# Cross-covariance attention on one core: the first V transfer moved behind the fourth unit of Q and K, and the first casts and transposes of V moved to later steps

## The chip, the core and the metric

The kernel runs on one core of a Trainium2 chip. A core has a matrix engine (TensorE, PE), a vector engine (VectorE, DVE), a scalar engine (ScalarE, ACT), a general one (GpSimd, POOL) and SyncE (SP), which here issues all DMA transfers. Each engine works through its own list of instructions in order and waits on semaphores for the others. The metric is device microseconds of one execution; before the change the median of five runs is 132.33 us.

## The reference

Q, K and V have shape 8 x 12 x 512 x 64 in float32: 96 heads, each with 512 rows of 64 numbers.

```python
Q_norm = Q / (np.linalg.norm(Q, axis=-2, keepdims=True) + 1e-10)
K_norm = K / (np.linalg.norm(K, axis=-2, keepdims=True) + 1e-10)
attn = np.einsum('bhnd,bhne->bhde', Q_norm, K_norm)
attn = np.exp(attn - np.max(attn, axis=-1, keepdims=True))
attn = attn / (np.sum(attn, axis=-1, keepdims=True) + 1e-10)
return np.einsum('bhnd,bhde->bhne', V, attn).astype(np.float32)
```

The attention matrix is one over features, 64 x 64 a head. It comes out of a sum over all 512 rows of Q and K, and V (512 x 64) is then multiplied by it.

## The kernel before

The heads are taken in 24 units of four heads. A unit of Q or of K is one transfer of 512 KB into a tile of 128 partitions. V comes in 12 transfers of 1 MB, numbered w, each holding two units; a V unit is numbered v. The output leaves in 512 KB stores, one for each unit (the last one in two halves). All loads and stores stand in one queue on SP, in the order in which the program calls load_qk (L69), load_v (L75) and store (L79). Up to eight transfers are in flight: from the ninth on, each waits for the landing of the one eight places ahead of it, and, where it reuses a buffer, for the engine that read it last.

The order of the work is written out by hand: the program has a manual schedule, and each engine runs its instructions in the order of the calls in the loop over steps (L229 to L258). In step s these parts stand one after another:

- load_qk for unit s + 3, V loads (L232) and stores (L235) as they come due
- cast_v (L89): a V unit is cast to bf16, one half on ACT and the other on DVE (L96, one instruction on each)
- cast_q (L82) for unit s + 1 on DVE
- normalise (L141) for unit s - 2: sum, reciprocal and multiply on DVE
- grams (L98) for unit s: 64 small matmuls on PE that give Q and K products and their squared norms together
- norms (L110): four DVE instructions that read the diagonal out of PSUM, and a power on POOL (L120); keep_kq (L105), a copy on ACT; scale_k (L122) on POOL
- logits (L129) for unit s - 1, four transposes on PE; scale_q (L133) on DVE; exps (L137) on ACT
- cast_k (L86) for unit s + 1 on DVE
- outs (L179): 16 matmuls on PE and two copies on ACT for an output unit; at most one a step, from step 4 on
- doubled (L173) for unit s - 2: a matmul on PE and a copy on ACT
- clear (L214), a copy of zeros on ACT, in the first steps
- vtrans (L149) for the V units that this step cast: eight transposes on PE into the one buffer of ps_v, and an evacuation on ACT (L159)

The number of outputs that should be done by step s is outs_by(s) (L62), the whole part of (s - 2) * 9 / 10. It is 0 up to step 3 and 1 at step 4. Before the change the V units to be cast in step s run from nt, the first not yet transposed, to n1 + 1, with n1 = outs_by(s) (L238); step 0 has none. So step 1 takes units 0 and 1, steps 2 and 3 take none, and step 4 takes unit 2. The first V load is called ahead of the loop (L227), the second in step 0 (L232).

After the loop a second one (L265 to L284) does the last six outputs; there four V units are transposed in float32 straight from the loaded tile (vtrans_f32, L161), and the copies are shared between ACT and DVE.

Of the kernel before, what the change touches and what calls it, by code (L numbers as in the profile page):

```python
# [27 lines left out]
def kernel(  # L28
# [10 lines left out]
    U = B * H // HU  # L39
# [22 lines left out]
    def outs_by(s):  # L62

        return max(0, (s - 2) * 9 // 10)
# [10 lines left out]
    def load_v(w):  # L75
        vf[w] = vp.tile([128, 2 * R * D], F32, name="vf")
        nc.sync.dma_start(out=vf[w], in_=Vf[w])

    def store(u, g=slice(0, SV)):  # L79
        nc.sync.dma_start(out=Of[u][:, g], in_=so[u][:, g].rearrange("p s t d -> p s (t d)"))  # L80
# [8 lines left out]
    def cast_v(v):  # L89

        w, i = divmod(v, 2)
        if i == 0:
            vb[w] = vbp.tile([128, A, TP, 2 * D], BF16, name="vb")
        x = vf[w].rearrange("p (a t d) -> p a t d", a=A, d=2 * D)
        for t, copy in ((2 * i, nc.scalar.copy), (2 * i + 1, nc.vector.tensor_copy)):
            copy(vb[w][:, :, t], x[:, :, t])  # L96
# [52 lines left out]
    def vtrans(v):  # L149

        w, i = divmod(v, 2)
        ps = ps_v.tile([128, A, 2, 128], BF16, name="vps")
        for t in range(2):
            for a in range(A):
                nc.tensor.transpose(ps[:, a, t, :], vb[w][:, a, 2 * i + t, :], identb)  # L155

        if i == 0:
            vt[w] = vtp.tile([128, TP, 128, A], BF16, name="vt")
        nc.scalar.copy(vt[w][:, 2 * i:2 * i + 2], ps.rearrange("p a t c -> p t c a"))  # L159
# [19 lines left out]
    def outs(u, copies=(nc.scalar.copy, nc.scalar.copy)):  # L179
        s = so[u] = sop.tile([128, SV, TP, 2 * D], F32, name="so")  # L180
        a = abuf[u % len(abuf)]
        v = vt[u // 2][:, :, u % 2 * 64:(u % 2 + 1) * 64]
        for g in range(SV):
            po = ps_o.tile([128, TP, 2 * D], F32, name="po")
            for t in range(TP):
                for x in range(2):
                    h = 2 * g + x
                    nc.tensor.matmul(  # L188
                        po[MV * x:MV * (x + 1), t, :], v[:, t, NP * h:NP * (h + 1), :].rearrange("p c a -> p (c a)"),
                        a[:, h].rearrange("p a d -> p (a d)"), tile_position=(0, MV * x),  # L190
                    )
            copies[g](s[:, g], po)  # L192
# [21 lines left out]
    def clear(i):  # L214

        nc.scalar.copy(abuf[i].rearrange("p h a d -> p (h a d)"), zeros)
# [4 lines left out]
    def on(f, u):  # L221
        if 0 <= u < U:
            f(u)

    on(cast_q, 0)
    on(cast_k, 0)
    load_v(0)  # L227
    nv, nst, nt = 1, 0, 0
    for s in range(U):  # L229
        n0, n1 = outs_by(s - 1), outs_by(s)  # L230
        on(load_qk, s + LOAD_AHEAD)
        while nv < min(U, n1 + 5) // 2:  # L232
            load_v(nv)
            nv += 1
        while nst < n1 - 3:  # L235
            store(nst)
            nst += 1
        new = range(nt, n1 + 2) if s >= 1 else ()  # L238
        for v in new:
            cast_v(v)  # L240
        on(cast_q, s + 1)
        on(normalise, s - 2)
        on(grams, s)
        on(norms, s)
        on(keep_kq, s)
        on(scale_k, s)
        on(logits, s - 1)
        on(scale_q, s - 1)
        on(exps, s - 1)
        on(cast_k, s + 1)  # L250
        for v in range(n0, n1):
            outs(v)
        on(doubled, s - 2)
        if 6 <= s + 5 < len(abuf):
            clear(s + 5)
        for v in new:
            vtrans(v)
            nt = v + 1  # L258
# [59 lines left out]
```

## Time and profile before

| | |
|---|---|
| median of 5 runs | 132.33 us (131.15 to 134.85) |
| profiled execution, own time | 133.27 us |
| its span, first to last instruction | 131.5 us |
| busy: DVE / ACT / PE / POOL | 95.8 / 91.5 / 90.5 / 64.1 us |
| moved by DMA | 50.67 MB, 385 GB/s over the span |
| first V transfer, from its issue to its landing | 9.97 us |
| V transfers, median from issue to landing | 12.5 us |
| mean granted clock of PE | 0.883 |

The profile is one execution. A row of the timeline gives the start in us from the span's start, the duration in us, the engine, the source line, the operation, what it writes and reads, the shapes, and the number of instructions merged into the row; in brackets stands how long the engine had been idle and what ended the wait. "SPq" rows are issues of transfers, not their movement. A landing can be read from SP: the issue of a transfer that was held up starts just after the landing of the one eight places ahead. Busy shares are averages over stages with different limits, so a wait counts only where nothing else lies beside it.

### The profile page before, as it was taken

What the parts mean: (1) busy time and instruction counts of PE and PEld (TensorE: products, weight loads), DVE (VectorE), ACT (ScalarE), POOL (GpSimd) and SP (SyncE); (2) the same over time, 40 slices, a digit from 0 to 9 for tenths busy, and PEclk for the clock granted to TensorE, in tenths of its full rate; (3) what the DMA queues carried; (4) which work ended last, traced back from release to release, by engine and by line L of the source; (5) the groups of instructions that cost most, each with busy time, mean ns of one, the idle gap of its engine ahead of it and who ended that gap; (6) DMA issues with size and microseconds to landing.
All of it is one profiled execution on the core that took longest, in us unless ns stands there. A gap on an engine that the chain in (4) does not pass through costs nothing.

```text
span 131.5 us, 5389 instructions
## 1 busy us (share of the span) xinstructions
PE 90.5 (69%) x2232; PEld 70.2 (53%) x2232; DVE 95.8 (73%) x366; ACT 91.5 (70%) x171; POOL 64.1 (49%) x57
## 2 busy tenths in 40 slices
PE   0146346779968759866994799682897758979630
PEld 0135244657846548644863587461675646867420
DVE  0460855898698996994798979983979698478840
ACT  7610564357899999994978288987689968677530
POOL 4023172698258882671668447763545657140000
PEclk9999999999999995995589658999779985699995
DMA  4999999999999999999999999999999999976775
GB/s 141 383 415 417 424 406 414 401 425 399 416 412 399 441 391 410 426 403 411 427 393 412 411 424 409 409 427 405 413 423 409 409 414 413 407 289 224 282 273 206
DMA packets 15208, 50.67 MB, mean 385 GB/s; under 512 B 1360, under 2 KB 1360, under 8 KB 13648
## 3 DMA queue, kind: packets, MB, share of 16 engines
q1 hardware_dynamic: 15184, 50.34, 95.8%
q8 instruction: 17, 0.28, 0.8%
q14 instruction: 7, 0.06, 0.1%
HBM read 37.75 MB, written 12.58 MB: 383 GB/s over the span
## 4 chain that ended last, share of the span: by engine, by line
PE 38%; DVE 22%; ACT 11%; issue 9%; DMA 8%; POOL 7%; SPq 2%; POOLq 0%; ACTq 0%; DVEq 0%
PE gram L103 16%; DVE scr L115 9%; DMA vf<-in_V_dram 8%; PE vps L155 7%; PE po L188 7%; POOL rq L120 5%; ACT so L192 3%; PE lgdup L176 3%; DVE sl L135 3%; PE lgdup L131 3%; ACT vt L159 3%; PE vps L170 2%; DVE qkb L87 2%; DVE qkb L84 2%; POOL kqs L125 1%
## 5 line engine op out<-in xcount | busy, mean ns | idle before, releaser
L120 POOL TENSOR_TENSOR rq<-nsq,mhalf 128x4 f32<-128x4 f32 x24 | 47.5, 1977 | 50.7 <-DVE nsq L115 42.1
L103 PE MATMUL gram<-qkb 32*128 32x128 bf16 x1536 | 37.1, 261 | 16.3 <-DVE qkb L87 8.6
L103 PEld LDWEIGHTS <-qkb 32*128 32x128 bf16 x1536 | 30.7, 117 | 23.2 <-DVE qkb L87 11.7
L115 DVE CUSTOM_DVE_ANT_0 scr<-gram,ident 128x128 f32<-128x128 f32 x96 | 22.1, 284 | 15.4 <-PE gram L103 15.3
L108 ACT COPY kq<-gram 64x256 f32<-64x256 f32 x24 | 8.8, 368 | 22.9 <-DVE nsq L115 22.7
L192 ACT COPY so<-po 128x512 f32<-128x512 f32 x42 | 22.8, 588 | 1.6 <-PE po L188 1.0
L159 ACT COPY vt<-vps 128x1024 bf16<-128x1024 bf16 x20 | 20.2, 1012 | 1.6 <-PE vps L155 1.1
L188 PE MATMUL po<-ab,vt 128*64 128x128 bf16 x384 | 19.6, 251 | 2.3 <-ACT vt L159 1.1
L84 DVE CAST qkb<-qf 128x1024 bf16<-128x1024 f32 x24 | 16.7, 696 | 5.4 <-DMA qf<-in_Q_dram 5.4
L155 PE MATMUL vps<-identb,vb 128*128 128x128 bf16 x160 | 15.4, 252 | 5.7 <-ACT vt L159 2.9
L188 PEld LDWEIGHTS <-vt 128*64 128x64 bf16 x384 | 14.4, 128 | 7.1 <-issue 4.3
L155 PEld LDWEIGHTS <-vb 128*128 128x128 bf16 x160 | 11.3, 113 | 12.7 <-ACT vb L96 4.5
L87 DVE CAST qkb<-kf 128x1024 bf16<-128x1024 f32 x24 | 16.2, 676 | 0.5 <-DMA kf<-in_K_dram 0.5
L125 POOL TENSOR_TENSOR kqs<-kq,rq 64x256 f32<-64x256 f32 x24 | 15.2, 632 | 1.9
L131 PE MATMUL lgdup<-ident,kqs 64*64 64x64 f32 x96 | 12.5, 267 | 4.5 <-POOL kqs L125 4.5
L96 ACT CAST vb<-vf 128x512 bf16<-128x512 f32 x20 | 12.3, 621 | 4.1 <-DMA vf<-in_V_dram 4.1
L176 PE MATMUL lgdup<-ab,identb 64*64 64x256 bf16 x24 | 7.5, 312 | 7.3 <-DVE sl L135 6.4
L131 PEld LDWEIGHTS lgdup<-ident,kqs 64*64 64x64 f32 x96 | 7.7, 131 | 8.7 <-POOL kqs L125 6.5
L96 DVE CAST vb<-vf 128x512 bf16<-128x512 f32 x20 | 8.3, 419 | 4.8 <-DMA vf<-in_V_dram 4.8
L139 ACT ACTIVATE ex<-sl 64x256 f32<-64x256 f32 x24 | 10.0, 417 | 2.0 <-DVE sl L135 1.3
L147 DVE TENSOR_TENSOR ab<-ex,rinv 64x256 bf16<-64x256 f32 x24 | 10.5, 437 | 0.8
L135 DVE TENSOR_TENSOR sl<-lgdup,rq 64x256 f32<-64x256 f32 x24 | 9.9, 411 | 1.1 <-PE lgdup L131 0.9
(21 smaller groups left out, 59.9 us busy)
## 6 DMA issues: line engine op xcount, KB each, us to landing
qf<-in_Q_dram SPq DMA_DIRECT2D x24, 512.0 KB, 11.2
kf<-in_K_dram SPq DMA_DIRECT2D x24, 512.0 KB, 11.2
vf<-in_V_dram SPq DMA_DIRECT2D x12, 1024.0 KB, 12.5
out_dram<-so SPq DMA_DIRECT2D x23, 512.0 KB, 11.2
out_dram<-so SPq DMA_DIRECT2D x2, 256.0 KB, 3.1
```

The source lines that it names most:

```text
L84: nc.vector.tensor_copy(qkb[u][:, :, 0:D], qf[u])
L87: nc.vector.tensor_copy(qkb[u][:, :, D:], kf[u])
L96: copy(vb[w][:, :, t], x[:, :, t])
L103: nc.tensor.matmul(gbuf[:, h, 0:2 * D], x, x, start=(t == 0), stop=(t == R - 1), tile_position=(NV * h, 0))
L115: nc.vector.tensor_tensor_reduce(out=scr, in0=gbuf[:, h, 0:2 * D], in1=ident, scale=1.0, scalar=1e-20, op0=ALU.mult, op1=ALU.add, accum_ou ...
L120: nc.gpsimd.tensor_tensor(out=r, in0=n2, in1=mhalf, op=ALU.pow)
L125: nc.gpsimd.tensor_tensor(out=kk[D:], in0=kq[u][D:], in1=rq[u][D:, :, None].to_broadcast([D, HU, D]), op=ALU.mult,)
L131: nc.tensor.transpose(lg[:, h, :], kqs[u][D:, h, :], ident[D:, D:])
L155: nc.tensor.transpose(ps[:, a, t, :], vb[w][:, a, 2 * i + t, :], identb)
L159: nc.scalar.copy(vt[w][:, 2 * i:2 * i + 2], ps.rearrange("p a t c -> p t c a"))
L188: nc.tensor.matmul(po[MV * x:MV * (x + 1), t, :], v[:, t, NP * h:NP * (h + 1), :].rearrange("p c a -> p (c a)"), a[:, h].rearrange("p a d ...
L192: copies[g](s[:, g], po)
```

## The change

The load of V 0 is no longer called ahead of the loop. In step 0 it is called after load_qk of unit 3, and no further V load is called until step 2. The V units to be cast are now limited by the step as well: step 2 takes unit 0, step 3 takes unit 1, and step 4 takes unit 2 as before.

```diff
     on(cast_q, 0)
     on(cast_k, 0)
-    load_v(0)
-    nv, nst, nt = 1, 0, 0
+    nv, nst, nt = 0, 0, 0
     for s in range(U):
         n0, n1 = outs_by(s - 1), outs_by(s)
         on(load_qk, s + LOAD_AHEAD)
-        while nv < min(U, n1 + 5) // 2:
+        while nv < (min(U, n1 + 5) // 2 if s >= 2 else 1):
             load_v(nv)
             nv += 1
         while nst < n1 - 3:
             store(nst)
             nst += 1
-        new = range(nt, n1 + 2) if s >= 1 else ()
+        new = range(nt, max(0, min(s - 1, n1 + 2)))
         for v in new:
             cast_v(v)
         on(cast_q, s + 1)
```

The order of the first transfers, before: Q/K 0, Q/K 1, Q/K 2, V 0, Q/K 3, V 1, Q/K 4, Q/K 5, Q/K 6. After: Q/K 0, Q/K 1, Q/K 2, Q/K 3, V 0, Q/K 4, Q/K 5, V 1, Q/K 6. On PE, the sixteen transposes of the first two V units stood between the logits of step 1 and gram 2; now eight stand ahead of gram 3 and eight ahead of gram 4. From step 4 on, each engine's list is the same as before.

## Prediction

> **What bounds the kernel now.** I read the page's rows in 40 slices first, then the table of waits, then the timeline around each wait for a load. On the page, the DMA rows and the queue that carries the data:
>
> ```profile
> DMA  4999999999999999999999999999999999976775
> GB/s 141 383 415 417 424 406 414 401 425 399 416 412 399 441 391 410 426 403 411 427 393 412 411 424 409 409 427 405 413 423 409 409 414 413 407 289 224 282 273 206
> ...
> q1 hardware_dynamic: 15184, 50.34, 95.8%
> ```
>
> From slice 2 to slice 35 (about 3.3 to 115 us; a slice is 131.5/40 = 3.29 us) the DMA engines never fall under nine tenths, and from slice 3 on they move about 410 GB/s. No compute engine is like that (DVE 73%, ACT 70%, PE 69%). All transfers stand in one SP queue in a fixed order, so when a load lands is set by the bytes ahead of it.
>
> The table of waits says where compute stood still for a load:
>
> ```profile
> DVE qkb L84 <- DMA qf<-in_Q_dram: 5.4, 2, 4.1
> DVE vb L96 <- DMA vf<-in_V_dram: 4.8, 2, 3.9
> ACT vb L96 <- DMA vf<-in_V_dram: 4.1, 1, 4.1
> ```
>
> Columns: total us, times, longest. For Q there are only the first transfer (4.1) and the second (1.25). For V there are two: 3.9 us on DVE with 4.1 on ACT, and a second on DVE of 0.9. The timeline places them. The first, in step 1, with what follows (start, duration, engine, line):
>
> ```profile
> 13.56 1.14 ACT L96 CAST vb<-vf 128x512 bf16<-128x512 f32 x2 [4.12 <-DMA vf<-in_V_dram]
> 13.56 0.76 DVE L96 CAST vb<-vf 128x512 bf16<-128x512 f32 x2 [3.92 <-DMA vf<-in_V_dram]
> ...
> 16.33 0.33 SPq L73 DMA_DIRECT2D kf<-in_K_dram  x1
> ...
> 17.60 0.33 SPq L72 DMA_DIRECT2D qf<-in_Q_dram  x1
> ...
> 18.21 1.01 PE L155 MATMUL vps<-identb,vb 128*128 128x128 bf16 x8 [2.94 <-ACT vt L159]
> ...
> 19.15 1.89 PE L103 MATMUL gram<-qkb 32*128 32x128 bf16 x64
> ```
>
> The second, in step 21, at the tenth V transfer (w = 9):
>
> ```profile
> 103.16 0.43 DVE L96 CAST vb<-vf 128x512 bf16<-128x512 f32 x1 [0.93 <-DMA vf<-in_V_dram]
> ...
> 103.50 1.10 DVE L84 CAST qkb<-qf 128x1024 bf16<-128x1024 f32 x1
> ...
> 104.53 0.40 DVE L143 TENSOR_REDUCE esum<-ex 64x4 f32<-64x256 f32 x1
> ...
> 105.51 0.28 DVE L115 CUSTOM_DVE_ANT_0 scr<-gram,ident 128x128 f32<-128x128 f32 x1
> ```
>
> This is the reading that decides. At 103.16 DVE had been idle for 0.93 us and started as V 9 landed. From there it works without a gap to the norms at 105.51, and the gram that these need was through at 104.43 (103.83 + 0.60). So the norms of step 21 are held by DVE's queue behind V 9, and through them the last 28 us. The chain that ended last follows PE there and doesn't print this, but the DVE rows are closed. The start of the last fifth of the kernel is pinned to a landing.
>
> **The change, part by part.** Order on SP. Before: Q/K 0 to 2, V 0, Q/K 3, V 1, Q/K 4, Q/K 5, Q/K 6. After: Q/K 0 to 3, V 0, Q/K 4, Q/K 5, V 1, Q/K 6. From the fifteenth transfer (Q 6) on, the order is the same, and 14 transfers with 8 MB stand ahead of it in both. No transfer is added, and the queue keeps eight in flight (from the ninth on each waits for the one eight places ahead, and both orders put at least 4 MB, some 10 us, into the engines). So every load from Q 6 to V 11, V 9 among them, keeps its landing: 0 us.
>
> When V 0 lands. In the old order it was seventh and landed at 13.54. In the new one it is ninth and ends the first 5 MB. The old order's ninth, K 3, ended the same 5 MB, and its landing shows in SP's issue eight places later: 17.60. Q 3 comes seventh, and transfers of 512 KB landed 1.27 us apart (Q 2 at 9.76, K 2 at 11.04), so about 12.3. Between 13.5 and 16.3 one such transfer took 2.7 us in place of 1.27 (V 0 at 13.54, SP's 16.33 for Q 3), as one packet of instructions of 1.09 us went through at 13.34. With this jump V 0 lands at 17.54, without it at 16.1, with a second one at 19.0. I take 17.54, the row with the same bytes.
>
> Here a rule speaks the other way. The Trainium skill, "DMA: Bandwidth & Descriptors" (Anatomy of one DMA), prices a DMA at about 2.0 us plus bytes over 436 GB/s: for 1 MB, 4.4 us. Issued at about 5.4, V 0 would by that estimate lie ready at 9.8, step 2 would wait for nothing, and the whole 3.9 us would be won at that place. But the formula is one transfer's own; the row has 9.97 us for V 0 seventh in the queue and a median of 12.5 for V. So V 0 is waited for in step 2.
>
> Step 1. Gone: two casts on ACT (1.14 together) and two on DVE (0.76), the wait ahead of them, sixteen transposes on PE (1.03 + 1.01), two evacuations on ACT (1.01 each), and the second group's 2.94 us wait for the single ps_v buffer. With rows of the same kind: cast of Q 2 at 9.76 as it lands, gram 1 ends at 11.6, norms to 12.5, scale_q to 12.8, cast of K 2 to 13.4, gram 2 on PE 13.45 to 15.3 (before: 19.15).
>
> Step 2. DVE and ACT both now have the cast of V unit 0 in front. ACT has been idle since 13.9, DVE since 13.4; both wait for 17.54. Queued behind it on DVE are cast_q 3, normalise 0, norms 2, scale_q 1 and cast_k 3; on ACT, keep_kq 2; gram 3 waits for them all. DVE: 17.54 + 0.42 + 0.68 + 1.1 (sum, reciprocal, multiply) brings norms 2 to 19.7; they end at 20.5, scale_q 1 at 20.9, cast_k 3 at 21.5. PE: doubled 21.0, eight transposes 21.4 to 22.4, gram 3 at 22.4. Before it stood at 23.01: a lead of 0.6.
>
> Step 3 had no V work before and now has a cast on each engine, eight transposes and an evacuation. DVE: 21.5 + 0.42 + 0.68 + 1.1 is 23.7; the norms wait for gram 3 to 24.3 and end at 25.2; scale_q 2 at 25.6, cast_k 4 at 26.2. PE: doubled after scale_q 2, to 26.0, transposes to 27.0, gram 4 at 27.05. Before: 27.01. The lead is spent: 0. ACT's evacuation ends at 28.0, and its first reader, outs 0, started at 30.06 before, so 2 us cover it. V 1 lands at 25.17 (the row of the old fourteenth, K 5), cast at 26.2: 1.0 us of cover. From step 4 on engine orders are equal.
>
> So the sum at step 4 is 0.0 us, with bounds from V 0's landing of -1.4 and +1.5. At V 9 a lead turns into a longer wait there: gain 0. A lag first eats the 0.93: at most 1.5 - 0.93 = 0.6 us is lost. I take 0. Against the profiled execution: span 131.5 + 0 and time 133.27 + 0; the 1.8 us around the span stays. The median shown, 132.33, is 0.9 under that execution, and I forecast it unchanged: 132.3. Five runs lie from 131.15 to 134.85, so differences within about 1% (1.3 us) can hardly be told from none.
>
> **Rivals.** Slower, by one mechanism, PE's clock. Step 2 leaves PE without work from 16.0 to 21.0, 5 us (logits 1 follow POOL's two steps: 12.5 + 2.26 + 0.61 is 15.4, and last 0.6). The skill, "TensorE: Matmul & The Clock Gate" (Part 1), says that after an idle window of about 3.4 us the array runs at half rate until it has been busy for about as long. Applied to a warm array this would cost grams 2 to 4 some 0.8 us each (1.89 at 19.15 against 1.07 at 98.70), 2.5 us. The row speaks against: all of grams 0 to 5 take 1.89 already, although the clock row prints nines there, so nothing is left to lose early. The place where it would hurt is the end. The granted clock was 0.50 from 107.4 to 114.2, and from 114.2 on the chain of the tail has some 7 us of matmuls at full clock. If steps shifted by fractions of a microsecond let the slow stretch last one window of 3.4 us longer, that window holds 1.7 us of matmuls on the chain (115.9 to 117.6), which double: 132.3 + 1.7 is 134.0. It decides from the moment when PE idles through a whole window at the wait for V 9. For it: the clock row swings between 5 and 9 all through the trace. Against: the pin holds the tail at the same time in both.
>
> Faster: the lead isn't lost at V 9, because the printed chain through PE is the true one. V 0's wait of 3.9 becomes one of 4.1 in DVE's row, so not that time is won but the 1.4 of an early V 0, with the 0.4 of the long cast at 103.50 (1.10 against 0.68): -1.8, 130.5. Against it: DVE has no gap from 103.16 to 105.51.
>
> That the change doesn't do what it says: the wait only moves from step 1 to step 2. That is my forecast for the early stage.
>
> **How the numbers follow.** Forecast 0.66, with a range of 131.3 to 133.3; slower by the clock or an unabsorbed lag 0.20, at 134.0 (lag alone 132.9); faster 0.14, at 130.5. Range 131.0 to 134.0. Chances: faster by over 1% 0.12, within 1% 0.67, slower by over 1% 0.21.
>
> **What would show it.** In the changed kernel: V's first cast on DVE and ACT waits about 4 us and starts near 17.5; gram 2 near 13.5, gram 4 near 27; Q 6 still lands near 26.4 and V 9 near 103.1 with a DVE wait in front of its cast; the GB/s row flat at 410 to slice 35. I am wrong if V 9 lands at another time, if DVE doesn't wait for it, or if the stretch from its landing to the end differs from 28.4 us by more than 1.

## The result, and the profile after

The changed kernel takes 132.21 us (median of 44 runs, 130.98 to 135.0) against 132.33 us (79 runs, 130.77 to 135.82). The ratio is 1.0008, with a 95% interval of 0.999 to 1.0026: no difference. Here and below a median is over all runs of a kernel, and a ratio over the runs that the comparison takes as undisturbed, so the two can differ by a few tenths of a percent.

The two profiled executions are not typical ones: they took 133.27 us before and 134.61 after, both above the medians (spans 131.5 and 132.8). Where those 1.3 us lie is looked at below. The page of the changed kernel, its DMA rows and the chain that ended last:

```profile
DMA  4999999999999999999999999999999999955775
GB/s 149 331 395 426 410 411 417 406 424 400 418 403 412 428 400 407 437 395 415 419 399 417 407 431 403 414 422 408 408 426 402 424 411 421 387 228 191 288 266 208
...
DMA 46%; PE 23%; DVE 11%; ACT 11%; issue 3%; SPq 3%; ACTq 0%
```

The chain of the kernel before:

```profile
PE 38%; DVE 22%; ACT 11%; issue 9%; DMA 8%; POOL 7%; SPq 2%; POOLq 0%; ACTq 0%; DVEq 0%
```

The transfers run as flat as before, to slice 35. The chain has changed: its share of DMA was 8% and is now 46%. It now runs through a transfer that in the kernel before lay just beside it. A piece of that chain in order of time (start, duration, what):

```profile
90.71 12.44 DMA vf<-in_V_dram
103.16 0.02 issue
103.18 0.43 DVE vb L96
103.61 0.60 DVE qkb L84
```

In the kernel before, DVE waited for V 9 as well. There PE was busy until 105.48, right up to the norms at 105.51, and so the chain was printed through PE. But what ended at 105.48 were output matmuls, which the norms don't read; the gram that they do read had ended at 104.43. The timeline of the changed kernel in the early steps (start, duration, engine, line; in brackets the idle time and what ended it):

```profile
17.60 0.62 ACT L96 CAST vb<-vf 128x512 bf16<-128x512 f32 x1 [2.88 <-DMA vf<-in_V_dram]
17.60 0.43 DVE L96 CAST vb<-vf 128x512 bf16<-128x512 f32 x1 [3.29 <-DMA vf<-in_V_dram]
...
22.10 1.89 PE L103 MATMUL gram<-qkb 32*128 32x128 bf16 x64
...
26.63 1.89 PE L103 MATMUL gram<-qkb 32*128 32x128 bf16 x64
```

The wait for V 0 stands one step later and is 0.6 us (DVE) to 1.2 us (ACT) shorter. Gram 3 starts 0.9 us earlier than before (23.01), gram 4 0.4 us earlier:

```profile
27.01 1.89 PE L103 MATMUL gram<-qkb 32*128 32x128 bf16 x64 [0.24 <-DVE qkb L87]
```

At the place of the second wait, first the kernel before and then the changed one:

```profile
101.56 0.67 DVE L87 CAST qkb<-kf 128x1024 bf16<-128x1024 f32 x1
```

```profile
100.40 0.67 DVE L87 CAST qkb<-kf 128x1024 bf16<-128x1024 f32 x1
...
103.18 0.43 DVE L96 CAST vb<-vf 128x512 bf16<-128x512 f32 x1 [2.10 <-DMA vf<-in_V_dram]
```

In the kernel before the wait was 0.93. The changed kernel arrives 1.16 us earlier, waits 1.17 us longer, and goes on at 103.18 in place of 103.16. V 9 is the last of three such places, though, and not the first. The first casts of V 7 and V 8, in the kernel before and then in the changed one:

```profile
83.79 0.41 DVE L96 CAST vb<-vf 128x512 bf16<-128x512 f32 x1
...
94.00 0.42 DVE L96 CAST vb<-vf 128x512 bf16<-128x512 f32 x1
```

```profile
83.12 0.43 DVE L96 CAST vb<-vf 128x512 bf16<-128x512 f32 x1 [1.84 <-DMA vf<-in_V_dram]
...
93.18 0.43 DVE L96 CAST vb<-vf 128x512 bf16<-128x512 f32 x1 [1.68 <-DMA vf<-in_V_dram]
```

V 7 landed at 83.14 before and 83.10 after, V 8 at 93.12 and 93.16. The kernel before came to both a little late and did not wait. The changed kernel came to V 7 at 81.28, 2.5 us ahead, and 1.84 of that was waited away on the spot. Between these landings, 10 us apart, DVE's own work takes 8.4 and 7.9 us, so it waits again at V 8 and at V 9. The change did win time, and waits for transfers took it back, most of it 20 us before V 9.

### The profile page after: what moved, and what is told of

The parts are those of the page before. It is cut to its first block, busy times and chain, and to the rows that moved or that the text cites. A ratio compares the mean times of both kernels' runs of the same rounds, so it can differ in the third digit from the quotient of the medians.

```text
span 132.8 us, 5389 instructions
## 1 busy us (share of the span) xinstructions
PE 90.6 (68%) x2232; PEld 70.4 (53%) x2232; DVE 95.3 (72%) x366; ACT 91.5 (69%) x171; POOL 63.4 (48%) x57
## 4 chain that ended last, share of the span: by engine, by line
DMA 46%; PE 23%; DVE 11%; ACT 11%; issue 3%; SPq 3%; ACTq 0%
DMA vf<-in_V_dram 19%; DMA kf<-in_K_dram 17%; DMA qf<-in_Q_dram 10%; PE gram L103 7%; PE po L188 5%; ACT so L192 4%; PE vps L155 4%; DVE scr L115 4%; PE vps L170 3%; ACT vt L159 3%; PE lgdup L176 2%; DVE sl L135 1%; SPq L73 1%; DVE qkb L84 1%; ACT ab L216 1%
## 5 line engine op out<-in xcount | busy, mean ns | idle before, releaser
L103 PE MATMUL gram<-qkb 32*128 32x128 bf16 x1536 | 36.2, 258 | 14.7 <-DVE qkb L87 10.3
L103 PEld LDWEIGHTS <-qkb 32*128 32x128 bf16 x1536 | 30.1, 115 | 20.0 <-DVE qkb L87 11.6
L84 DVE CAST qkb<-qf 128x1024 bf16<-128x1024 f32 x24 | 16.3, 680 | 6.7 <-DMA qf<-in_Q_dram 6.7
L188 PE MATMUL po<-ab,vt 128*64 128x128 bf16 x384 | 19.1, 246 | 2.5 <-ACT vt L159 1.4
L155 PE MATMUL vps<-identb,vb 128*128 128x128 bf16 x160 | 15.9, 259 | 0.7 <-ACT vb L96 0.7
L125 POOL TENSOR_TENSOR kqs<-kq,rq 64x256 f32<-64x256 f32 x24 | 14.7, 611 | 1.9
```

The costliest lines, as they stand in the source:

```text
L84: nc.vector.tensor_copy(qkb[u][:, :, 0:D], qf[u])
L103: nc.tensor.matmul(gbuf[:, h, 0:2 * D], x, x, start=(t == 0), stop=(t == R - 1), tile_position=(NV * h, 0))
L125: nc.gpsimd.tensor_tensor(out=kk[D:], in0=kq[u][D:], in1=rq[u][D:, :, None].to_broadcast([D, HU, D]), op=ALU.mult,)
L188: nc.tensor.matmul(po[MV * x:MV * (x + 1), t, :], v[:, t, NP * h:NP * (h + 1), :].rearrange("p c a -> p (c a)"), a[:, h].rearrange("p a d ...
```

## The experiments

Two theories were put against each other. By the pin theory the end follows the landing of V 9, and what is won or lost ahead of it shows only as the length of DVE's wait there. By the rival a chain of compute sets the end, and the change was neutral because its gains and costs cancelled in the early steps.

### The casts late, the transfers as before

```diff
 (kernel before)
-        new = range(nt, n1 + 2) if s >= 1 else ()
+        new = range(nt, max(0, min(s - 1, n1 + 2)))
```

> V's transfers as in the kernel before (V 0 lands near 13.5), only the casts and transposes moved to steps 2 and 3. Pin theory (the end follows the landing of V 9): no engine waits for V 0 any more, gram 4 stands up to 3 us ahead of 27.0, and all of that turns up as a longer wait of DVE for V 6 to V 9 (at V 9 over 2 us instead of 0.93); V 9 lands at 103.1 as before and the time is 132.2, within 0.5. Rival (the chain of compute decides, and the change was neutral only because what it won and lost in the early steps cancelled): the 3.9 us wait is gone and nothing was put in its place, so about 3 us faster, 129.3.

Measured: 132.16 us, ratio 0.9992 (0.9961 to 1.0024). The early wait is all but gone, and there are long ones at V 7, V 8 and V 9, of which the first and the last are shown:

```profile
14.05 0.43 DVE L96 CAST vb<-vf 128x512 bf16<-128x512 f32 x1 [0.19 <-DMA vf<-in_V_dram]
```

```profile
83.05 0.43 DVE L96 CAST vb<-vf 128x512 bf16<-128x512 f32 x1 [1.99 <-DMA vf<-in_V_dram]
...
103.21 0.43 DVE L96 CAST vb<-vf 128x512 bf16<-128x512 f32 x1 [1.92 <-DMA vf<-in_V_dram]
```

The first row is from step 2, the last from step 21. Gram 4 stood at 25.38, 1.6 us ahead, and gram 6 at 33.44, 3.1 us ahead (36.54 in the kernel before). DVE came to V 7 still 2.7 us ahead, and from there on it kept the pace of the landings. The 3.9 us wait of step 1 is all but removed, and the time is the same. The rival's 129.3 is ruled out. So is 130.6, which the rival would give with the 1.6 us that were there at gram 4.

### The transfers late, the casts as before

```diff
 (changed kernel)
-        new = range(nt, max(0, min(s - 1, n1 + 2)))
+        new = range(nt, n1 + 2) if s >= 1 else ()
```

> V's transfers as in the changed kernel (V 0 lands near 17.5), but both V units cast in step 1 as before. Pin theory: DVE and ACT stand until 17.5 in step 1, gram 2 and all that follows is about 4 us later; the slack of 0.93 at V 9 takes the first part, so the loss is 3.1 us at most, less what the steps make up on the way: 134 to 135.4. Rival (chain of compute): the full 4 us, 136.3.

Measured: 134.22 us, ratio 1.0187 (1.0133 to 1.0242). Here the early wait is 7.33 us on DVE, and at V unit 18 DVE no longer waits:

```profile
17.07 0.76 DVE L96 CAST vb<-vf 128x512 bf16<-128x512 f32 x2 [7.33 <-DMA vf<-in_V_dram]
```

```profile
104.90 0.41 DVE L96 CAST vb<-vf 128x512 bf16<-128x512 f32 x1
```

Gram 4 stands at 30.53, 3.5 us late. At V unit 18 DVE is 1.74 us late (104.90 against 103.16), and the median is 2.0 us over that of the kernel before in the same session (132.20). So of the 3.5 us, 0.93 went into the slack, 0.85 was made up on the way, and 1.74 arrived at V unit 18. The late transfers alone cost 1.9%; the late casts, which come with them in the change, make up for it.

### V 9 one step later

```diff
 (changed kernel)
-        while nv < (min(U, n1 + 5) // 2 if s >= 2 else 1):
+        while nv < (min(U, n1 + 5) // 2 if s >= 2 else 1) and (nv, s) != (9, 19):
```

> The changed kernel with V 9 called one step later, so behind Q/K 23 in the queue: it lands 3.75 us later (106.9 instead of 103.16), everything else in the queue earlier or equal. Pin theory: the DVE wait in front of the cast of V unit 18 grows to 5 to 6 us and the end moves by 3.7 us, to 135.9. Rival (chain of compute through PE, V 9 has room): 1 us or less.

Measured: 135.93 us, ratio 1.033 (1.0264 to 1.0396).

```profile
107.75 0.43 DVE L96 CAST vb<-vf 128x512 bf16<-128x512 f32 x1 [5.71 <-DMA vf<-in_V_dram]
```

One transfer out of 85 was moved three places back. It came 4.6 us later in this profile, DVE waited 5.71 us for it, and the median rose by 3.7. This is the most direct of the runs: the end does follow V 9.

### Each V load ahead of the Q and K of its step

```diff
 (changed kernel)
-        on(load_qk, s + LOAD_AHEAD)
+        if s < 12:
+            on(load_qk, s + LOAD_AHEAD)
         while nv < ...:
             load_v(nv)
             nv += 1
+        if s >= 12:
+            on(load_qk, s + LOAD_AHEAD)
```

> The changed kernel with each V load ahead of, not behind, the Q/K load of its own step from step 12 on: V 7, V 8 and V 9 land 2.5 us earlier, the Q/K of those steps 2.5 us later. Pin theory: the lead of 1.2 to 2.1 us that was waited away is kept until Q 22 (landing near 102) is the next to pin; DVE casts V unit 18 near 101.5 and the end comes 1.0 to 1.5 us earlier, 130.9. Rival (chain of compute): no change, 132.2.

Measured: 131.06 us, ratio 0.9942 (0.9917 to 0.9967).

```profile
100.70 0.56 DVE L96 CAST vb<-vf 128x512 bf16<-128x512 f32 x1 [1.28 <-DMA vf<-in_V_dram]
101.80 0.69 DVE L84 CAST qkb<-qf 128x1024 bf16<-128x1024 f32 x1 [0.54 <-DMA qf<-in_Q_dram]
```

V 7 and V 8, which moved forward as well, are not waited for any more (casts at 80.36 and 90.90). The pin moves 2.5 us forward with V 9, and right behind it Q 22 is the next one. The tile that DVE casts at 101.80 starts 1.7 us earlier than before (103.50), and the median falls by 1.14 us. The last row is the limit that had been named.

### The same swap on the kernel before

```diff
 (kernel before: the same edit)
```

> The kernel before with the same swap as the run with each V load ahead of the Q/K load of its own step (from step 12 on). Pin theory: in the kernel before only 0.93 us was waited away at V 9, so at most that comes out: 131.3, and the early change, worth nothing without the swap, is worth 0.2 to 1 us with it (131.06 measured for the changed kernel with the swap). Rival (the swap helps in some other way, for instance by the order of stores): the same gain as in the changed kernel, 1.1 us, to 131.1.

Measured: 131.66 us, ratio 0.9938 (0.991 to 0.9967). The median is 0.8 us under that of the kernel before in the same session (132.46), within the 0.9 that I had set as the most. But the ratio is the changed kernel's (0.9938 and 0.9942), so the 0.2 to 1 us that the early change was to be worth with the swap do not show: the two intervals leave room for about half a microsecond either way. In its profile DVE casts V unit 18 at 100.71 and Q 22 at 101.24, with no wait shown at either; Q 22 had landed at 101.22. So this execution came to the same limit, by its own pace. Up to step 12 it ran the same lists as the profiled kernel before, and still its gram 6 stood at 34.71 in place of 36.54: the 0.93 us was the wait of one execution, not a constant of the kernel. That the gain is the same is what the rival said, and no run here tests its reason (the order of the stores). A direct comparison of both kernels with the swap was not made.

### A known delay on DVE, in both kernels

```diff
+    spare = const.tile([128, R, D], BF16, name="spare")
...
+        for _ in range(2 if s == 10 else 0):
+            nc.vector.tensor_copy(spare, qf[s + 1])
         on(normalise, s - 2)
```

> The kernel before with two more copies of a Q tile on DVE (0.69 us each, 1.38 in all) in step 10; their output is not used. Pin theory: the slack of 0.93 at V 9 takes the first part, about 0.4 us are lost, 132.6. Rival (chain of compute): all of it, 133.6.

> The changed kernel with the same two copies (1.38 us) in step 10. Pin theory: DVE waited 2.10 us for V 9, the wait shrinks to about 0.7 and the time stays, 132.2. Rival (chain of compute): 133.6.

Measured, the kernel before with the delay: 132.63 us, ratio 0.9968 (0.9936 to 1.0). The changed kernel with it: 132.34 us, ratio 0.9984 (0.9952 to 1.0016). The copies are in the profiles with 0.69 us each, and 1.38 us more work on DVE, the busiest engine, costs nothing in either. The row of step 21 in the kernel before with the delay, and then in the changed one with it:

```profile
103.40 0.43 DVE L96 CAST vb<-vf 128x512 bf16<-128x512 f32 x1 [0.30 <-DMA vf<-in_V_dram]
```

```profile
103.62 0.43 DVE L96 CAST vb<-vf 128x512 bf16<-128x512 f32 x1 [2.80 <-DMA vf<-in_V_dram]
```

In the first, the wait shrank from 0.93 to 0.30 and 0.4 us of loss, which I had expected, can't be seen. In the second, the wait was longer than without the delay (2.80 against 2.10), and I had looked at the wrong wait: the copies run at 51 us, ahead of V 7 and V 8, where this kernel had already given up its lead. From the cast of V 8 to the arrival at V 9 DVE took 7.90 us with the delay and without it; the added 0.7 is the queue's, which brought V 8 earlier (92.89 against 93.16) and V 9 later (103.59 against 103.16). The wait where the delay should show did not shrink either:

```profile
82.92 0.43 DVE L96 CAST vb<-vf 128x512 bf16<-128x512 f32 x1 [2.07 <-DMA vf<-in_V_dram]
```

DVE came to V 7 at 80.85 with 1.38 us of added work, and at 81.28 without it. So the way there differs by 1.8 us between these two executions for other reasons, and their profiles can't show the delay. The times can: the rival's 133.6 is ruled out twice.

### The stores later as well

On top of the swap, each store of the main loop is called two units later, and the ones left over follow behind the last V load.

```diff
-        while nst < n1 - 3:
+        while nst < n1 - 5:
...
-        store(u - 3)
+        while nst < u - 2:
+            store(nst)
+            nst += 1
```

> The changed kernel with the V loads first and with every store of the main loop called for two units later (n1 - 5 in place of n1 - 3), so that two stores (1.3 us each) fewer stand ahead of V 9 and Q/K 23; the stores left over come behind the last V load. Pin theory: V 9, Q 22 and Q 23 land up to 2.6 us earlier than with V first alone, the compute follows as far as its own pace allows (its waits there were 1.3 and 0.7 us), and the end comes 0.5 to 1.5 us earlier than 131.06: 130.0. Rival (after the swap compute is the bound): no change, 131.1.

> The kernel before with both later edits (V loads first from step 12 on, stores two units later), so that it differs from the run with the same two edits on the changed kernel (130.99) by the early change alone. Pin theory: with both edits the transfers run without a gap to the last store, so the end follows the queue and the early order is again worth nothing: 131.0, within 0.3. Rival (with the pins gone compute decides and the early lead counts): 0.5 to 1.2 us slower than that, 131.5 to 132.2.

Measured, the changed kernel with both edits: 130.99 us (130.75 to 132.49 over 18 runs), ratio 0.992 (0.9887 to 0.9953). The kernel before with both: 131.35 us (130.63 to 134.64 over 22), ratio 0.9954 (0.9928 to 0.9979). The page of the first:

```profile
DMA  4999999999999999999999999999999999999991
GB/s 138 387 421 421 406 410 416 409 416 405 415 412 402 425 393 413 425 405 428 396 412 406 430 402 417 414 416 403 422 419 401 421 412 409 403 405 388 348 371 54
```

The DMA engines are now full to the last slice but one. The 130.0 that I had expected was not reached, for two reasons that the trace shows. V 9 landed at 97.68, yet DVE cast it at 100.43, only 0.3 us earlier than with the swap alone and without a wait: from there compute is the slower one. And the last store, issued at 122.89, landed at 128.08: now the queue holds the end. This version is the fastest of the study, but its interval overlaps that of the swap alone. Whether the early change counts here (130.99 against 131.35) the intervals don't tell either: 131.35 lies between what the two theories had said for it (130.7 to 131.3, and 131.5 to 132.2). What the pin theory rested on there is not in the profile, of an execution of 132.68 us: DVE came to V 9 only at 102.03, 4 us after its landing at 97.96.

### PE kept busy during the wait for V 9

```diff
 (changed kernel)
         on(grams, s)
+        for t in range(R if s == 21 else 0):
+            for h in range(HU):
+                x = qkb[s][NV * h:NV * (h + 1), t, :]
+                nc.tensor.matmul(gbuf[:, h, 256:256 + 2 * D], x, x, start=True, stop=True, ...)
```

> The changed kernel with 64 more small matmuls on PE directly behind gram 21 (the same operands as that gram, written to columns of its PSUM banks that nothing reads), in the time in which DVE and PE wait for V 9 and for what follows it. They add 1.1 to 1.9 us of work to PE where it stood idle for 2.4. Clock theory (what the slower rival rests on: the wait for V 9 lets the granted clock of PE drop, and the tail then runs slow): with the wait filled the clock from 110 to 117 us is near 1.0 in place of 0.50, the stretch from V 9's landing to the end is 26.5 to 27.5 us in place of 29.6, and the median falls by 0.5 to 1 us below the changed kernel's, to 131.5. If the clock's slow stretches come from elsewhere: the same time or up to 0.5 us longer, 132.2 to 132.7, with the same spread of single runs.

Measured: 135.34 us, ratio 1.0243 (1.0175 to 1.0311), so 2.9 us worse than the kernel before in the same session (132.47). The granted clock of PE from 110 to 117 us was 0.99, as the clock theory has it (0.50 in the changed kernel's profile), and all the same the stretch from V 9 to the end took 31 us. The timeline shows what came in:

```profile
112.04 0.74 PE L103 MATMUL gram<-qkb 32*128 32x128 bf16 x40
115.00 0.52 PE L103 MATMUL gram<-qkb 32*128 32x128 bf16 x24 [2.22 <-issue]
...
115.56 0.29 DVE L115 CUSTOM_DVE_ANT_0 scr<-gram,ident 128x128 f32<-128x128 f32 x1 [2.66 <-PE gram L103]
```

PE stops in the middle of gram 23 and waits 2.22 us for nothing that the profile names; a packet of 16 KB of instructions had started at 112.62. In gram 22 there is such a stop of 1.06 us. The profile of the changed kernel has no stop of this kind over 0.5 us after V 9. The added matmuls are 128 more instructions for PE with their weight loads. That they moved waits for more program into the grams that DVE waits for fits these rows, but no run tests it. So the run doesn't answer its question: the clock was high in this place, but what that is worth at the end of this kernel was not measured.

## Why the prediction was right

**The queue.** Every load from Q 6 on was to keep its landing. Q 6 landed at 26.43 before and 26.45 after, V 9 at 103.14 and 103.16. One load did not: V 6 landed at 69.07 before and 70.81 after, for a reason that is open; by V 7 the landings agree again. V 0 was put at 17.54 by counting bytes; it landed at 17.57. That it came so close is luck: in the six other profiles with V 0 in this place it landed between 16.90 and 17.87. And the jump of 1.46 us in the landings, which I had put between 13.5 and 16.3 us, was not there as one piece: V 0's own 1 MB took 2.99 us, 0.45 more than two transfers of 1.27, and Q 1 came 0.95 us late (8.16 against 7.21), and so gram 1 and gram 2 were 0.7 and 0.9 us later than forecast (10.39 and 14.36). By the ninth transfer the sums agree again. The rule for a single transfer (4.4 us for 1 MB) would have had V 0 there long before step 2; DVE did wait for it, until 17.60. The Trainium skill, "DMA: Bandwidth & Descriptors" (Anatomy of one DMA), moreover fits that rule to transfers issued by GpSimd, while those of this kernel are issued by SP, which the prediction left unsaid.

**Steps 2 and 3.** Forecast were gram 3 at 22.4 and gram 4 at 27.05, a lead of 0. They stood at 22.10 and 26.63, a lead of 0.4. In the profiles of the five experiments that have the same lists up to step 10 the lead at gram 4 is 0.6 to 1.6, so the forecast of 0 is at the low end. The order of the waits was as described, and DVE's steps took what the rows of before had said.

**A term that was missing.** Between gram 4 and gram 5 the lead grew from 0.4 to 1.4 us, and at gram 6 it was 1.85. The first row is gram 5 in the kernel before, the second gram 5 after:

```profile
32.38 1.89 PE L103 MATMUL gram<-qkb 32*128 32x128 bf16 x64
```

```profile
30.96 1.07 PE L103 MATMUL gram<-qkb 32*128 32x128 bf16 x64
```

The gap to 1.4 has two parts. The first, 0.65 us, is there at the logits of step 4, where PE waited for POOL before and not after (POOL's power took 2.72 us in that step before and 1.78 after):

```profile
29.50 0.63 PE L131 MATMUL lgdup<-ident,kqs 64*64 64x64 f32 x4 [0.60 <-POOL kqs L125]
```

```profile
28.45 0.63 PE L131 MATMUL lgdup<-ident,kqs 64*64 64x64 f32 x4
```

The second is PE's clock, whose first record in the trace stands at 35.74 us before and at 30.50 after, both at full clock. So the eight transposes in front of gram 5 took 0.67 us in place of 1.03, and gram 5 itself 1.07 in place of 1.89. In all seven profiles with the late casts gram 5 or gram 4 is the first to take 1.07, in four of the five with the early casts it is gram 6. That the new order, in which the transposes of steps 2 and 3 stand right against the grams, is the reason was only argued; in the fifth (the swap on the kernel before) gram 3 already took 1.07 and gram 6 stood 1.8 us early, so an execution can get there without the new order. The prediction carried the lead at step 4 as if no step after it could change, which was wrong by a whole microsecond or more, and harmless, since any lead ends at a landing. With a sum that ended at step 4 and no pin I would have forecast the same number for a bad reason.

**The pin.** The decisive step was to read DVE's row at 103.16 against the printed chain, which ran through PE there. What the prediction did not see is that the lead would be taken at V 7 and V 8 before it came to V 9: in the profile before, these two landings have no wait, and DVE was only 0.65 and 0.88 us behind them. The mechanism was right, the first place of it was not named. The run with V 9 late (+3.7 us for one transfer moved), the casts late (no gain for a wait removed) and the two delays (no loss for work added) show it from three sides. The price of a lag was right in kind and a little high: 3.5 us late at gram 4 became 2.0 at the end, where the whole lag less 0.93 would be 2.6.

**The slower rival, and a sign that failed.** I had said that the stretch from V 9's landing to the end should stay 28.4 us, within 1. In the profiled execution it was 29.6. The table by stretches, from V 9's cast to the end, of the kernel before, and then of the changed one (us, busy time of each engine, granted clock, DMA share, GB/s):

```profile
103.16:131.50 28.34, 18.30 (x354) 14.31 (x353) 19.00 (x59) 17.13 (x33) 7.38 (x7) 0.82 0.83 321
```

```profile
103.18:132.80 29.62, 19.69 (x321) 15.27 (x317) 18.76 (x59) 15.72 (x31) 7.09 (x6) 0.71 0.80 313
```

DVE and ACT did no more work, PE did its work at a clock of 0.71 in place of 0.82: the clock was 0.50 from 107.42 to 114.25 us before, and from 105.60 to 119.25 after. That is what the rival had named, with 1.3 us near the 1.7 that it was given, though two executions don't show that the clock is the cause. It isn't an effect of the change: the medians are equal, and the run with the casts late, which is pinned at the same time (103.21), needed only 26.5 us for the stretch, with the clock at 0.99 from 110 to 117 us against 0.70 and 0.50 in these two. The two delay runs, pinned at 103.40 and 103.62, needed 28.0 us at 0.76 and 27.1 at 0.81. So five executions lie in the order of their clocks in that window, which was chosen after the fact; the one run aimed at the clock (0.99, and 31 us) was spoilt by something else. What moves the clock from one execution to the next is open.

## What to carry to other kernels

Where a saturated DMA queue has a fixed order, ask for each wait at the front which landing further back will collect what it gives: once compute is at a transfer before it lands, a further saving ahead of it only lengthens the wait. Several such transfers can follow one another, and the first takes the lead won at the start; a wait at a later one tells of the stretch since the one before it, not of the start. Look for them in the rows of the engines, not only in the printed chain, which follows the latest release and can pass a pin by a fraction of a microsecond. And the pin tells where to work: the swap of a few loads at the end won 0.6%, where removing a wait of 3.9 us at the start had won nothing.

## What the runs showed of the hardware

Landings on one queue kept to the bytes ahead of them: V 9 landed between 103.14 and 103.59 us in the profiles of all seven kernels that leave its place in the queue alone. It isn't so for each load: V 6 landed between 69.07 and 71.05 in the same seven. Compute's way to a landing was less even than V 9: DVE came to V 7 at 81.28 in the changed kernel, and at 80.85 with 1.38 us of work added.

PE can stop within a run of matmuls for 1 to 2.6 us with no wait that the profile names, beside a packet of 16 KB of instructions on another queue. In the twelve profiles there are 14 such stops of over 2 us in the grams, and each begins within 0.4 us of the start of such a packet; most packets (17 or 18 in a profile) have no long stop beside them. The Trainium skill, "Runtime: NRT & Kernel Launch" (Instruction fetch mechanics), describes such a stream of 16 KB blocks and holds its cost to be mostly hidden; if these stops are waits for a block, which the profile doesn't name, it was not hidden here. In the kernel before, this row waited 2.57 us with such a packet at 89.48:

```profile
91.93 0.23 PE L103 MATMUL gram<-qkb 32*128 32x128 bf16 x4 [2.57 <-issue]
```

Whether such a stop costs anything depends on what it falls into. In the filler run two of them, 3.3 us together, lie in grams that DVE waits for, and that run was 2.9 us slower than the kernel before.

The clock row of the page printed nines for the first 30 us in both kernels, while the grams there took 1.89 us and not 1.07. The first clock record is at 35.74 us before and 30.50 after, and the duration of a known matmul group is the better reading.
